# Where the split of silu(gate)*up stands among the weights' splits, and 256 bytes in the place of the sums

## The chip, the cores and the metric

The kernel runs on one core of a Trainium2 chip. The metric is the time of one execution on the device, in microseconds (us). The engines are PE (TensorE, matrix products), DVE (VectorE), ACT (ScalarE), POOL (GpSimd) and SP (SyncE, which here issues the loads). PEld stands for PE's loading of the stationary operand.

## The reference

Two layers act on 256 tokens of width 2048, all in float32. A layer is a mixer (a gated recurrence and two kinds of attention, projected back) and a feed-forward part; the change lies in the second.

```python
for l in range(DEPTH):                      # 2
    ...
    x = x + mix @ w_out[l]
    h = rmsnorm(x, g_ffn[l])
    x = x + (jax.nn.silu(h @ w_gate[l]) * (h @ w_up[l])) @ w_down[l]
return rmsnorm(x, g_final)
```

`w_gate` and `w_up` are 2048 x 5632, `w_down` is 5632 x 2048.

## The kernel before

**Products in three parts.** A float32 product is made of three faster ones: each operand is split into a high part (a cast, `fp32r`) and a low part (the operand less its high part), and `mm3` (lines 234 to 236) adds high x high, high x low and low x high. So each weight tile that arrives from memory in a raw buffer (`wraw`, 6 buffers) is cast by ACT (`whi`, line 228) and subtracted by DVE (`wlo`, line 229) in `load_split`, with 3 buffers for the two parts (`whl_p`). Every activation is split likewise (`split_scaled`: ACT line 399, DVE line 400).

**The feed-forward part.** The 5632 columns are worked in blocks of 512, 11 to a layer, in groups of 4, 4 and 3. A block is one call of `gate_up`; after a group, its part of the down product (`gemm` with `w_down`) is added to `x`. There are 22 blocks in all.

**A block** runs over the 2048 rows in 8 pairs of 256.

- The *ordinary part* takes the first five pairs (`NORD`): 24 products of 128x512 each, `acc<-whi,xTh` and the like in the profile.
- The *sums part* takes the last three pairs with a Strassen-like scheme, seven `mm3` in place of eight. ACT and DVE form sums of the gate's and the up's weights (lines 340 to 343, into raw buffers) and split them into the arena (ACT lines 338, 339, 346, 348; DVE 344, 345, 347, 349). There are two sets of such places, used in turn, `a = p % 2 * SET` (line 329), each of 7168 elements. The seven products go to banks named P1, C11, C12, P5, P7, P6 and C21, in this order. P5, P7 and P6 are taken from a pool of three PSUM banks, `aux` (line 325).
- At its end DVE and ACT form silu(gate)*up from the banks (lines 356 to 380) into `sil`.

**`hidden`** (line 965) turns `sil` into the down product's stationary operand `hT`. For each half it takes an `aux` bank, lets PE make four 128x128 transposes into it (line 393), and splits the bank into `hTh` (ACT, line 399) and `hTl` (DVE, line 400). It is a side job: `run` calls `tick` after each pair of whatever runs next, and `hidden` waits two ticks, so the two halves come after the third and the fourth pair of the next block. After the last block of a group they come after the third and fourth tile of the down product.

**What sets the order of work.** PE's order is written out by hand (`manual_schedule`, line 1015): it is the order of the program text with its ticks. The orders of ACT and DVE are chosen when the program is built, among the instructions that are ready by then, by priority: those within `tc.high_priority(offset=AHEAD)` go ahead of the others, and among equals the earlier in the text. The weights' splits (line 227), the sums (line 337) and the block's closing steps have this priority; `hidden` has not. Each engine then works through its own order without a change on the chip.

The pool that matters:

```python
aux_p = pool("aux", 3, space=PSUM)                 # line 69
P5, P7, P6 = (aux() for _ in range(3))             # line 325
```

Of the kernel before, what the change touches and what calls it, by code (L numbers as in the profile page):

```python
# [21 lines left out]
P = 128  # L22
D = 2048
T = 256
NT = 2
# [8 lines left out]
AHEAD = 100000  # L34
# [23 lines left out]
def body(ctx: ExitStack, tc: tile.TileContext, x_in, pos_in, pvec_in, lamv_in, cst_in, w_in, w_r, w_i, w_q_b,  # L58
# [78 lines left out]
    A_ON = A_RG + 1024 + 1536  # L137
    A_DQ = A_QT

    SET = 7168  # L140
    A_SIL = ARENA1
    A_U = A_SIL + 1024

    def at(a, *shape):
        n = math.prod(shape)
        v = ar1[0][:, a:a + n] if a < ARENA1 else ar2[:, a - ARENA1:a - ARENA1 + n]
        if len(shape) == 2:
            v = v.rearrange("p (a b) -> p a b", a=shape[0])
        elif len(shape) == 3:
            v = v.rearrange("p (a b c) -> p a b c", a=shape[0], b=shape[1])  # L150
        return v
# [54 lines left out]
    def load(src_ap, kk, shape, raw=None):  # L206

        n = kk * math.prod(shape)
        if raw is None:
            raw = wraw_p.tile([P, CHUNK], F32, name="wraw")  # L210
        if len(shape) == 1:
            last_load[:] = [nc.sync.dma_start(raw[:, :n].rearrange("p (k c) -> p k c", k=kk),
                                              src_ap.rearrange("(k p) c -> p k c", p=P))]
        else:
            rv = raw[:, :n].rearrange("p (k h e) -> p k h e", k=kk, h=shape[0])
            sv = src_ap.rearrange("(k p) h e -> p k h e", p=P)
            for k in range(kk):
                nc.sync.dma_start(rv[:, k], sv[:, k])
        return raw
# [78 lines left out]
    def gate_up(wg, wu, rs, sil):  # L298
# [3 lines left out]
        fl = lambda v: v.rearrange("p a b -> p (a b)")  # L302
# [10 lines left out]
        for p in range(NORD):  # L313
            ks = (2 * p, 2 * p + 1)
            hl = [load_split(w[2 * p * P:(2 * p + 2) * P], 2, (512,)) for w in (wg, wu)]
            for s, t in ((0, 0), (1, 1), (0, 1), (1, 0)):
                hi, lo = hl[s]
# [8 lines left out]
        n = KD // 2  # L326
        for p in range(NORD, n):
            ks = (2 * p, 2 * p + 1)
            a = p % 2 * SET
            G, U = (load(w[2 * p * P:(2 * p + 2) * P], 2, (512,)).rearrange("p (a b) -> p a b", a=2)  # L330
                    for w in (wg, wu))
            V, W = (wraw_p.tile([P, CHUNK], F32, name="wraw").rearrange("p (a b) -> p a b", a=2) for _ in range(2))
            gh, gl = at(a, 2, 512), at(a + 1024, 2, 512)
            uh, ul = at(a + 2048, 512), at(a + 2560, 512)
            vh, vl = at(a + 3072, 2, 512), at(a + 4096, 2, 512)
            wh, wl = at(a + 5120, 2, 512), at(a + 6144, 2, 512)
            with tc.high_priority(offset=AHEAD):
                nc.scalar.copy(fl(gh), fl(G))  # L338
                nc.scalar.copy(uh, U[:, 1])
                tt(V[:, 0], U[:, 0], G[:, 0], ALU.subtract)  # L340
                tt(V[:, 1], U[:, 1], U[:, 0], ALU.subtract)  # L341
                tt(W[:, 0], U[:, 1], V[:, 0], ALU.subtract)  # L342
                tt(W[:, 1], G[:, 1], W[:, 0], ALU.subtract)  # L343
                tt(fl(gl), fl(G), f_(fl(gh)), ALU.subtract)  # L344
                tt(ul, U[:, 1], f_(uh), ALU.subtract)  # L345
                nc.scalar.copy(fl(vh), fl(V))  # L346
                tt(fl(vl), fl(V), f_(fl(vh)), ALU.subtract)
                nc.scalar.copy(fl(wh), fl(W))  # L348
                tt(fl(wl), fl(W), f_(fl(wh)), ALU.subtract)  # L349
            first, end = p == NORD, p == n - 1  # L350
            q = p - NORD
            S = [(xSh[:, q, i], xSl[:, q, i]) for i in range(4)]
            mm3(P1, xp(ks[0], 0), (gh[:, 0], gl[:, 0]), first, end)
            if end:
                with tc.high_priority(offset=AHEAD):
                    nc.scalar.copy(sil[1], P1)
            mm3(C11, xp(ks[1], 0), (gh[:, 1], gl[:, 1]), False, end)
            if end:
                with tc.high_priority(offset=AHEAD):
                    tt(sil[0], sil[1], C11, ALU.add)  # L360
                    nc.scalar.activation(sil[0], sil[0], AF.Silu, scale=rs[:, 0:1])
            mm3(C12, S[3], (uh, ul), False, end)
            mm3(P5, S[0], (vh[:, 0], vl[:, 0]), first, end)
            mm3(P7, S[2], (vh[:, 1], vl[:, 1]), first, end)
            mm3(P6, S[1], (wh[:, 0], wl[:, 0]), first, end)
            if end:
                with tc.high_priority(offset=AHEAD):
                    tt(u2, sil[1], P6, ALU.add)
                    tt(u3, u2, P7, ALU.add)
            mm3(C21, xp(ks[1], 1), (wh[:, 1], wl[:, 1]), False, end)  # L370
            if end:
                with tc.high_priority(offset=AHEAD):
                    tt(sil[1], u3, C21, ALU.add)
                    nc.scalar.activation(sil[1], sil[1], AF.Silu, scale=rs[:, 1:2])
                    tt(u2, u2, P5, ALU.add)
                    tt(u2, u2, C12, ALU.add)
                    tt(u3, u3, P5, ALU.add)
                    tt(u3, u3, o22, ALU.add)
                    for t, u in ((0, u2), (1, u3)):
                        nc.vector.scalar_tensor_tensor(sil[t], u, rs[:, t:t + 1], sil[t], ALU.mult, ALU.mult)  # L380
            yield
# [7 lines left out]
    def transposed(dsts, srcs):  # L389

        ps = aux()
        for d, s in zip(dsts, srcs):
            nc.tensor.transpose(ps[:, d:d + P], s, ident)  # L393
        return ps

    def split_scaled(hi, lo, src, g):

        if g is None:
            i = nc.scalar.copy(hi, src)
            nc.vector.tensor_tensor(lo, src, hi.bitcast(F32), ALU.subtract)  # L400
        else:
            i = nc.scalar.activation(hi, src, AF.Copy, scale=g)
            nc.vector.scalar_tensor_tensor(lo, src, g, hi.bitcast(F32), ALU.mult, ALU.subtract)  # L403
        return i
# [161 lines left out]
    def layer(l, rs):  # L566
# [3 lines left out]
        fl = lambda v: v.rearrange("p b t -> p (b t)")  # L570
# [231 lines left out]
        for i in range(4):  # L802
            h = ht_p.tile([P, 4, T], F32R, name="hTh")
            lo = ht_p.tile([P, 4, T], F32R, name="hTl")
            for j in range(4):

                k = (list(range(10, 16)) + list(range(6)) + list(range(6, 10)))[i * 4 + j]
# [148 lines left out]
        for f0, f1 in ((0, 4), (4, 8), (8, 11)):  # L956
            hT = []
            for f in range(f0, f1):
                sil = [at(A_SIL + t * 512, 512) for t in range(NT)]
                fs = slice(f * 512, (f + 1) * 512)  # L960
                run(gate_up(w_gate[l][:, fs], w_up[l][:, fs], rs[0], sil))
                h = ht_p.tile([P, 4, T], F32R, name="hTh")
                lo = ht_p.tile([P, 4, T], F32R, name="hTl")

                def hidden(sil=sil, h=h, lo=lo):
                    yield 2
                    for k in range(0, 4, 2):
                        ps = transposed([0, 128, 256, 384],
                                        [sil[t][:, (k + j) * P:(k + j + 1) * P] for j in range(2) for t in range(NT)])
                        split_scaled(fl(h[:, k:k + 2]), fl(lo[:, k:k + 2]), ps, None)  # L970
                        yield
                add(hidden())
                for j in range(4):
                    hT.append((h[:, j, :], lo[:, j, :]))
            last = f1 == 11
            if end and last:
                take(F32)
                gf = at(0, D)
                nc.sync.dma_start(gf, g_final.to_broadcast([P, D]))
            for cg in range(2):  # L980
                fin = end and last and cg == 1

                def ev(s, t, g, ps):
                    c = cg * 1024 + g * 512
                    nc.vector.tensor_tensor(x[:, t, c:c + 512], x[:, t, c:c + 512], ps, ALU.add)
                    if last:
                        sumsq(ss[:, t, cg * 2 + g:cg * 2 + g + 1], x[:, t, c:c + 512])
                    if end and last and cg == 0:
                        nc.vector.tensor_tensor(x[:, t, c:c + 512], x[:, t, c:c + 512], gf[:, c:c + 512], ALU.mult)
                    if fin and g == 1:  # L990
                        finish(t, ss, gf)
                run(gemm(lambda k: hT[k],
                         [(w_down[l][f0 * 512:f1 * 512, cg * 1024:(cg + 1) * 1024], [(0, 512), (512, 512)])],
                         [[k] for k in range(4 * (f1 - f0))], ev, last=3 if fin else 0))
                drain()
                if last and not end:
                    add(xT_steps("g_mix", l + 1, cg * 8, cg * 8 + 8))
# [62 lines left out]
```

## Time and profile before

| | |
|---|---|
| median of 3 runs | 2241.07 us (2236.26 to 2241.4) |
| the profiled execution's own time | 2241.19 us |
| its span, first to last instruction | 2239.4 us |
| mean granted clock of TensorE | 0.974 |
| moved by DMA | 391.17 MB, mean 175 GB/s |

The profile is of one execution. Its time is 1.8 us above its span, and within 0.2 us of the median. A group's line counts instructions of one line of the code; "idle before" is the time in which the engine had nothing to do just before them, and the releaser is the work whose end let them go. In the rows of a window stand the stretch and its length, then for PE, PEld, DVE, ACT and POOL the busy time (and the count of instructions), then the granted clock as a share of full speed, the mean busy share of the DMA engines and what they moved.

### The profile page before, as it was taken

The numbers are of one execution on the slowest core, as the hardware profiler recorded it, in microseconds if no ns is written. First come the engines' busy times: TensorE is split into PE (matmuls) and PEld (weight loads), VectorE is DVE, ScalarE is ACT, GpSimd is POOL, SyncE is SP. The second block draws the span as 40 slices with busy tenths as digits, with TensorE's granted clock in tenths as the row PEclk, the third lists the DMA queues.
The fourth block names the chain that finished last, engine by engine and source line by source line (L and its number), as shares of the span: only waits on it lengthen the run. The fifth ranks groups of instructions, "written<-read, shape, count | busy, mean of one in ns | idle before, by whom it ended". The sixth has DMA issues, their size and how long they took to land.

```text
span 2239.4 us, 27021 instructions
## 1 busy us (share of the span) xinstructions
PE 2108.8 (94%) x10104; PEld 1761.2 (79%) x10104; DVE 1545.2 (69%) x2115; ACT 1136.2 (51%) x1541; POOL 14.9 (1%) x32
## 2 busy tenths in 40 slices
PE   8999999888998889988999999998889988899888
PEld 8899887777887778877898898877778877788776
DVE  5775658777477774777566756587764877648775
ACT  5854656444354443444447545564543554434444
POOL 0000000000000000000000000000000000000000
PEclk9999999999999999999999999999999999999999
DMA  7564555545664555554565645654556645565553
GB/s 240 167 184 132 170 182 160 175 160 170 193 199 162 169 168 190 180 195 150 175 189 159 179 149 163 183 169 151 173 184 191 195 160 160 186 191 191 169 191 133
DMA packets 183220, 391.17 MB, mean 175 GB/s; under 512 B 18960, under 2 KB 36384, under 8 KB 182960
## 3 DMA queue, kind: packets, MB, share of 16 engines
q1 hardware_dynamic: 183040, 389.36, 54.9%
q8 instruction: 79, 1.29, 0.2%
q14 instruction: 53, 0.43, 0.1%
q0 software_dynamic: 48, 0.09, 0.0%
HBM read 387.30 MB, written 2.10 MB: 174 GB/s over the span
## 4 chain that ended last, share of the span: by engine, by line
PE 69%; DVE 17%; DMA 8%; issue 4%; ACT 2%; SPq 0%; DVEq 0%; POOLq 0%; POOL 0%; ACTq 0%
PE acc L235 20%; PE acc L234 20%; PE acc L236 20%; DMA wraw<-in_w_up 5%; DVE wlo L229 4%; PE aux L234 2%; DVE arena L344 2%; PE aux L235 2%; PE aux L236 2%; DVE arena L349 2%; ACT whi L228 1%; PE aux L393 1%; DVE arena L345 1%; DVE wraw L342 1%; DVE wraw L343 1%
## 5 line engine op out<-in xcount | busy, mean ns | idle before, releaser
L229 DVE TENSOR_TENSOR wlo<-wraw,whi 128x1024 fp32r<-128x1024 f32 (+2 forms) x608 | 716.1, 1182 | 451.5 <-ACT whi L228 446.2
L228 ACT CAST whi<-wraw 128x1024 fp32r<-128x1024 f32 (+2 forms) x608 | 618.7, 1019 | 728.4 <-PE acc L236 536.2
L235 PE MATMUL acc<-wlo,xTh 128*128 128x512 f32 (+1 forms) x1200 | 465.7, 388 | 11.3 <-DVE wlo L229 11.2
L234 PE MATMUL acc<-whi,xTh 128*128 128x512 f32 (+1 forms) x1200 | 471.1, 393 | 0.0
L236 PE MATMUL acc<-whi,xTl 128*128 128x512 f32 (+1 forms) x1200 | 463.5, 386 | 0.0
L234 PE MATMUL acc<-whi,hTh 128*128 128x512 f32 (+1 forms) x992 | 388.2, 391 | 0.0
L236 PE MATMUL acc<-whi,hTl 128*128 128x512 f32 (+1 forms) x992 | 384.7, 388 | 0.0
L235 PE MATMUL acc<-wlo,hTh 128*128 128x512 f32 (+1 forms) x992 | 384.4, 387 | 0.0
L235 PEld LDWEIGHTS acc<-wlo,xTh 128*128 128x128 f32 x1200 | 225.5, 188 | 65.7 <-DVE wlo L229 23.0
L234 PEld LDWEIGHTS acc<-whi,xTh 128*128 128x128 f32 x1200 | 225.4, 188 | 43.9 <-ACT whi L228 0.5
L236 PEld LDWEIGHTS acc<-whi,xTl 128*128 128x128 f32 x1200 | 225.3, 188 | 44.1
L234 PEld LDWEIGHTS acc<-whi,hTh 128*128 128x128 f32 x992 | 186.4, 188 | 37.8 <-issue 1.3
L236 PEld LDWEIGHTS acc<-whi,hTl 128*128 128x128 f32 x992 | 186.2, 188 | 37.9
L235 PEld LDWEIGHTS acc<-wlo,hTh 128*128 128x128 f32 x992 | 186.4, 188 | 36.4
L234 PE MATMUL aux<-arena,xSh 128*128 128x512 f32 x198 | 83.1, 420 | 100.6 <-DVE hTl L400 76.0
L234 PEld LDWEIGHTS aux<-arena,xSh 128*128 128x128 f32 x198 | 38.8, 196 | 114.1 <-ACT whi L228 93.2
L234 PE MATMUL acc<-xTh,whi 128*128 128x256 f32 x384 | 111.1, 289 | 1.7 <-ACT whi L228 1.0
L235 PE MATMUL acc<-xTl,whi 128*128 128x256 f32 x384 | 108.8, 283 | 1.6 <-DVE xTl L403 1.6
L236 PE MATMUL acc<-xTh,wlo 128*128 128x256 f32 x384 | 108.6, 283 | 0.5 <-DVE wlo L229 0.5
L346 ACT CAST arena<-wraw 128x1024 fp32r<-128x1024 f32 x66 | 69.3, 1049 | 47.6 <-DVE wraw L341 47.4
L344 DVE TENSOR_TENSOR arena<-wraw,arena 128x1024 fp32r<-128x1024 f32 x66 | 80.7, 1223 | 14.4 <-ACT arena L338 13.8
L348 ACT CAST arena<-wraw 128x1024 fp32r<-128x1024 f32 x66 | 69.4, 1051 | 36.3 <-DVE wraw L343 28.7
(230 smaller groups left out, 2614.5 us busy)
## 6 DMA issues: line engine op xcount, KB each, us to landing
wraw<-in_w_gate SPq DMA_DIRECT2D x176, 512.0 KB, 4.4
wraw<-in_w_up SPq DMA_DIRECT2D x176, 512.0 KB, 4.6
wraw<-in_w_down SPq DMA_DIRECT2D x176, 512.0 KB, 4.3
wraw<-in_w_out SPq DMA_DIRECT2D x64, 512.0 KB, 3.8
wraw<-in_w_in SPq DMA_DIRECT2D x48, 512.0 KB, 4.0
wraw<-in_w_in SPq DMA_DIRECT2D x48, 384.0 KB, 3.2
wraw<-in_w_in SPq DMA_DIRECT2D x32, 416.0 KB, 3.5
arena<-in_w_in SPq DMA_DIRECT2D x16, 384.0 KB, 7.4
```

What stands on the lines that cost most here:

```text
L228: nc.scalar.copy(hi[:, :n], raw[:, :n])
L229: nc.vector.tensor_tensor(lo[:, :n], raw[:, :n], hi[:, :n].bitcast(F32), ALU.subtract)
L234: nc.tensor.matmul(ps, a[0], b[0], start=start, stop=False)
L235: nc.tensor.matmul(ps, a[0], b[1], start=False, stop=False)
L236: nc.tensor.matmul(ps, a[1], b[0], start=False, stop=stop)
L342: tt(W[:, 0], U[:, 1], V[:, 0], ALU.subtract)
L343: tt(W[:, 1], G[:, 1], W[:, 0], ALU.subtract)
L344: tt(fl(gl), fl(G), f_(fl(gh)), ALU.subtract)
L345: tt(ul, U[:, 1], f_(uh), ALU.subtract)
L346: nc.scalar.copy(fl(vh), fl(V))
L348: nc.scalar.copy(fl(wh), fl(W))
L349: tt(fl(wl), fl(W), f_(fl(wh)), ALU.subtract)
```

## The change

It does two things. `hidden`'s transposes and splits are put within the same high priority that the weights' splits have. And the two sets of sums in the arena begin 64 elements (256 bytes) later: `a` goes from 0 and 7168 to 64 and 7232, counted from the arena's start; the arena has 14,504 elements.

```diff
--- before.py
+++ after.py
@@ -137,7 +137,7 @@
     A_ON = A_RG + 1024 + 1536
     A_DQ = A_QT
 
-    SET = 7168
+    A_SET, SET = 64, 7168
     A_SIL = ARENA1
     A_U = A_SIL + 1024
 
@@ -326,7 +326,7 @@
         n = KD // 2
         for p in range(NORD, n):
             ks = (2 * p, 2 * p + 1)
-            a = p % 2 * SET
+            a = A_SET + p % 2 * SET
             G, U = (load(w[2 * p * P:(2 * p + 2) * P], 2, (512,)).rearrange("p (a b) -> p a b", a=2)
                     for w in (wg, wu))
             V, W = (wraw_p.tile([P, CHUNK], F32, name="wraw").rearrange("p (a b) -> p a b", a=2) for _ in range(2))
@@ -965,9 +965,11 @@
                 def hidden(sil=sil, h=h, lo=lo):
                     yield 2
                     for k in range(0, 4, 2):
-                        ps = transposed([0, 128, 256, 384],
-                                        [sil[t][:, (k + j) * P:(k + j + 1) * P] for j in range(2) for t in range(NT)])
-                        split_scaled(fl(h[:, k:k + 2]), fl(lo[:, k:k + 2]), ps, None)
+                        with tc.high_priority(offset=AHEAD):
+                            ps = transposed([0, 128, 256, 384],
+                                            [sil[t][:, (k + j) * P:(k + j + 1) * P] for j in range(2)
+                                             for t in range(NT)])
+                            split_scaled(fl(h[:, k:k + 2]), fl(lo[:, k:k + 2]), ps, None)
                         yield
                 add(hidden())
                 for j in range(4):
```

## Rows read from the trace of the kernel before

**Rows 1.** Page, part 1: busy us (share of the span) x instructions of each engine

```profile
PE 2108.8 (94%) x10104; PEld 1761.2 (79%) x10104; DVE 1545.2 (69%) x2115; ACT 1136.2 (51%) x1541; POOL 14.9 (1%) x32
```

**Rows 2.** Waits: engine, line, what it waited for: us in total, times, longest

```profile
PE aux L234 <- DVE hTl L400: 76.0, 12, 7.3
...
PE aux L234 <- ACT whi L228: 24.6, 4, 6.6
```

**Rows 3.** Groups by shape: instructions xcount | busy us, mean ns | idle before, releaser

```profile
L229 DVE TENSOR_TENSOR wlo<-wraw,whi 128x1024 fp32r<-128x1024 f32 x508 | 619.0, 1223 | 401.0 <-ACT whi L228 396.4
L228 ACT CAST whi<-wraw 128x1024 fp32r<-128x1024 f32 x508 | 533.9, 1052 | 632.9 <-PE acc L236 500.9 <-issue 59.8 <-DMA wraw<-in_w_gate 21.1
...
L234 PE MATMUL aux<-arena,xSh 128*128 128x512 f32 x198 | 83.1, 420 | 100.6 <-DVE hTl L400 76.0 <-ACT whi L228 24.6
...
L344 DVE TENSOR_TENSOR arena<-wraw,arena 128x1024 fp32r<-128x1024 f32 x66 | 80.7, 1223 | 14.4 <-ACT arena L338 13.8
...
L348 ACT CAST arena<-wraw 128x1024 fp32r<-128x1024 f32 x66 | 69.4, 1051 | 36.3 <-DVE wraw L343 28.7 <-PE acc L236 5.4
...
L400 DVE TENSOR_TENSOR hTl<-aux,hTh 128x512 fp32r<-128x512 f32 x44 | 30.1, 685 | 0.0
...
L399 ACT CAST hTh<-aux 128x512 fp32r<-128x512 f32 x44 | 25.4, 578 | 0.0
```

**Rows 4.** Timeline, 404 to 425 us: start, us, engine, instruction [idle before, releaser]

```profile
406.64 0.60 PE L393 MATMUL aux<-ident,arena 128*128 128x128 f32 x4
...
409.28 0.58 ACT L399 CAST hTh<-aux 128x512 fp32r<-128x512 f32 x1
...
409.70 0.69 DVE L340 TENSOR_TENSOR wraw<-wraw 128x512 f32<-128x512 f32 x1 [0.18 <-DMA wraw<-in_w_up]
...
415.72 0.39 PE L236 MATMUL aux<-arena,xSl 128*128 128x512 f32 x1
416.12 0.69 DVE L340 TENSOR_TENSOR wraw<-wraw 128x512 f32<-128x512 f32 x1
...
420.27 1.23 DVE L347 TENSOR_TENSOR arena<-wraw,arena 128x1024 fp32r<-128x1024 f32 x1
...
421.40 0.69 DVE L400 TENSOR_TENSOR hTl<-aux,hTh 128x512 fp32r<-128x512 f32 x1
...
422.24 0.77 PE L234 MATMUL aux<-arena,xSh 128*128 128x512 f32 x1 [6.13 <-DVE hTl L400]
```

**Rows 5.** Window 409.70 to 421.40, DVE alone: busy us (instructions), clock, DMA share, GB/s

```profile
409.70:421.40 11.70, 11.70 (x15) 0.99 0.60 182
```

**Rows 6.** Timeline around a wait put down to line 228, 808.9 to 810.2 us

```profile
809.02 0.69 DVE L400 TENSOR_TENSOR hTl<-aux,hTh 128x512 fp32r<-128x512 f32 x1
...
809.86 0.76 PE L234 MATMUL aux<-arena,xSh 128*128 128x512 f32 x1 [6.02 <-ACT whi L228]
```

**Rows 7.** Windows around the first wait: us, five engines' busy us, clock, DMA share, GB/s

```profile
416.10:422.24 6.14, 0.01 (x2) 0.03 (x1) 6.14 (x10) 3.14 (x3) 0.00 (x0) 0.90 0.78 220
422.24:427.90 5.66, 5.66 (x13) 4.44 (x14) 4.57 (x4) 2.09 (x2) 0.00 (x0) 0.50 1.04 378
```

**Rows 8.** Windows: sums parts of the 16 blocks with the wait, first and sum

```profile
412.55:435.86 23.31, 17.18 (x65) 13.67 (x63) 15.43 (x19) 9.07 (x10) 0.00 (x0) 0.85 0.63 211
...
sum 364.68, PE 264.11 PEld 210.92 DVE 249.23 ACT 146.81 POOL 0.00; mean PE 16.51 PEld 13.18 DVE 15.58 ACT 9.18 POOL 0.00
```

**Rows 9.** Windows: sums parts without it, first of a layer, and sum of four others

```profile
365.47:381.12 15.65, 14.57 (x65) 11.75 (x63) 14.59 (x23) 10.34 (x13) 0.00 (x0) 1.00 0.58 188
...
sum 57.11, PE 57.11 PEld 47.31 DVE 55.35 ACT 37.51 POOL 0.00; mean PE 14.28 PEld 11.83 DVE 13.84 ACT 9.38 POOL 0.00
```

**Rows 10.** Windows: ordinary parts after ten with, four without, and a layer's first

```profile
sum 282.57, PE 282.57 PEld 232.37 DVE 233.21 ACT 154.98 POOL 0.00; mean PE 28.26 PEld 23.24 DVE 23.32 ACT 15.50 POOL 0.00
...
sum 117.55, PE 114.77 PEld 92.62 DVE 99.48 ACT 63.40 POOL 0.00; mean PE 28.69 PEld 23.16 DVE 24.87 ACT 15.85 POOL 0.00
...
381.12:412.55 31.43, 29.26 (x130) 22.99 (x129) 26.69 (x32) 17.15 (x20) 0.00 (x0) 1.00 0.59 187
```

## The prediction

> **What bounds the kernel now.** I read the page's first part, then the waits, then the groups of the long wait, then the order in time around one of its occurrences, then all occurrences side by side. The first part puts PE at 94% of the span, DVE at 69% and ACT at 51% [rows 1]: PE carries the time, and its idle 130 us are the place to look. The waits say that most of that idle time stands in one place, PE's `aux` product of line 234: 12 waits for the split `hTl` of line 400, 76.0 us, and 4 put down to line 228, 24.6 us [rows 2]; its group shows the same 100.6 us [rows 3]. That is 16 waits of 6.3 us.
>
> The order in time shows what one of them is [rows 4]. PE runs the three pairs of the Strassen-like part (below "the sums part") from 412.55. After P5 and P7 of the first pair, at 415.72, comes P6, which takes the third `aux` bank. That bank still holds the second four transposes of the block before, made at 406.64. ACT copied them to `hTh` at 409.28, but DVE subtracts them to `hTl` only at 421.40: fifteen instructions of the next two pairs' sums stand in DVE's order ahead of it, from L340 at 409.70 to L347 at 420.27 [rows 5]. PE starts again at 422.24, 0.15 us after `hTl` ends. The four waits put down to line 228 are the same: at 809.86 PE starts 0.15 us after an `hTl` that began at 809.02 and took 0.69 [rows 6]. So all 16 end with this one instruction.
>
> The wait costs more than its idle time. Cutting that block into stretches, the granted clock is 0.90 on the mean while PE is idle and 0.50, the lower of its levels of 1.2 and 2.4 GHz, for the 5.66 us after it [rows 7]. So the whole of the sums part is the right measure. The 16 blocks with the wait take 364.68 us, 22.79 each, at a clock of 0.85 [rows 8]. In the first block of a group no earlier block has left transposes, and the wait is missing: four of the six such blocks take 57.11 us, 14.28 each, at a clock of 1.00, all of it PE's busy time [rows 9]. The other two, the first of each layer, take 15.65.
>
> **The change, part by part.**
>
> *Priority of `hidden`.* It adds and removes no instruction. PE's order is written by hand, so the transposes stay where they are; 44 `hTh` copies (0.58 us) and 44 `hTl` splits (0.69 us) [rows 3] get the standing of the weights' splits. In ACT's order they already sit next to the transposes (409.28 against 406.64 [rows 4]). In DVE's order `hTl` should go from 421.40 to right behind `hTh`, near 410. The instructions that it passes, of two pairs, start one `hTl`, at most 0.69 us, later. They issue no DMA; what SP issues when DVE frees a raw buffer is later by that 0.69 too, and POOL has no work here. Then P6's bank is free some 5 us before PE asks for it, PE doesn't stop, and the clock doesn't fall. Each block saves 22.79 - 14.28 = 8.51 us, of which 6.3 is idle time and 2.2 the low clock: 16 x 8.51 = **136.2 us**.
>
> *What is late next.* Without the wait DVE and the DMAs lose the time in which they got ahead. Is the last pair's data there? DVE doesn't stop during the wait, so its times hold: `vl` of the third pair (L347) is done at 420.27 + 1.23 = 421.50. PE, without a stop, would want it at 412.55 + 2 x 4.76 + 3 x 0.68 = 424.1 (4.76 is a third of 14.28, 0.68 a seventh of that). Slack 2.6 us, less the 0.69 that `hTl` takes. Nothing new stops PE there, as in the free blocks.
>
> After that comes the next block's ordinary part, with less lead. After a block with the wait it takes 28.26 us (282.57 over 10); after a free block 117.55 over 4, 29.39 [rows 10], because the weights' low parts come late behind the block's closing sums. Ten of the 16 blocks are followed by a further block: 10 x 1.13 = **11.3 us** given back. Six are followed by the down product, where PE has twelve products of 0.227, 2.7 us, for each new weight tile: I take nothing, and keep 6 x 1.13 = 6.8 us as the bound.
>
> A page speaks against the whole gain. The Trainium skill, "Perfetto Trace Analysis", section "Optimization Strategy", reads a gap that repeats on the engine that should be saturated as a possible sign that SBUF or PSUM is too small for the next tile. By that reading three `aux` banks are too few, a new order alone leaves the gap, and the time stays. The trace says otherwise to me: a free bank here lacks only a subtraction whose input was there 11.5 us before.
>
> *The 256 bytes.* Nothing in the trace of before shows a cost of where the sums lie. The casts and splits into the sums take 1051 (L348) and 1223 ns (L344), those into the weight tiles 1052 (L228) and 1223 (L229) [rows 3]. PE's 63 products that read the sums take 14.28 / 63 = 0.227 us each in a free block; five ordinary pairs have 120 products from the weight tiles and two sets of transposes of 0.60 [rows 4] in 28.26: 0.226. A difference of 3 ns on some 400 such instructions would be 1 us, so I take 0, and keep 1 us either way. The last set now ends at element 14,400 of the arena's 14,504, so it runs into nothing.
>
> **Sum.** 2239.4 - 136.2 + 11.3 = 2114.5 us of span; the profiled execution's own time is 1.8 above its span and 0.1 above the median of the runs: **2116 us**, 5.6% less.
>
> **The rivals.**
>
> *The wait moves to the weights.* DVE is close to full, and every block now follows a fast one. The dearest case in the trace is the first block of a layer, where DVE starts with no lead: 15.65 [rows 9] and then 31.43 [rows 10], in place of 14.28 and 29.39. If every block were so: 10 x 3.41 + 6 x 1.37 = 42 us back, 2158. For it: DVE is busy 55.35 of 57.11 us in the free blocks [rows 9]. Against it: in the ordinary part it is busy 99.48 of 117.55 [rows 10], so it can catch up in each block, and the loads ran at 378 GB/s when they had to [rows 7].
>
> *The order doesn't change, or the banks are too few whichever it is.* The placing of `hTl` is decided when the program is built, by a model of the engines' times; if there it isn't ready before the sums, it stays late. Then 2241. That would need `hTh` late too, and it isn't: it is there 2 us after the transposes. The skill's reading above would give this time as well.
>
> *Slower: ACT or DVE stands waiting for the transposes.* `hTh` and `hTl` are put into ACT's and DVE's order ahead of the next pair's casts, PE reaches the transposes later than the model thought, and the casts queue behind. Its place is the end of the third and fourth ordinary pair. After each transpose PE then waits for `hTh`, `whi` and `wlo` in turn, 0.58 + 1.05 + 1.22 = 2.85 us [rows 3], twice a block: 5.7. The sums start without lead, and DVE needs 6.42 us for a pair (from L340 at 409.70 to L340 at 416.12 [rows 4]) against PE's 4.76: 1.6 late at the last pair, and two splits of 1.13 (from L347 at 420.27 to the next start at 421.40) behind it, 2.3. Together 9.6 us a block, 154 us: 2116 + 154 = 2270. It decides from 7.8 us a block (124.9 / 16) on. Against it: ACT shows no wait before `hTh` in the rows, and the sums of a later pair are begun at 409.70, ahead of PE's first product with any at 412.55. The Trainium skill, "PSUM — Partial Sum Buffer", section "Engine vs sequencer instructions", says that ScalarE's and VectorE's queues are strictly first in, first out, which is what this case needs; the fifteen instructions ahead of a ready `hTl` agree.
>
> **How the numbers follow.** The forecast has 0.76, the wait that moves 0.15, no change 0.05, slower 0.04. A measurement of this kernel can tell about 0.3% from no change. Faster by more is the first two, 0.91; same 0.05; slower 0.04. The range goes from the sum without what is given back (2105), with 5 us of room for the sums' place and the small waits elsewhere, 2100, to the moved wait with the down products' 6.8 us, 2165. It leaves out the last two cases and little more.
>
> **What would show it.** In the new profile `hTl` starts within some 5 us of the transposes. The group of line 234 with `aux` and `xSh` has under 10 us of idle time, from 100.6. The 16 sums parts take 14.3 to 15 us, at a clock of 1.00. The ordinary parts take 29 to 30. PE is busy near 98%. The casts and splits of the sums keep 1051 and 1223 ns. It is wrong if `hTl` is early and the sums parts still take over 16 us, or the ordinary parts over 31 (the wait has moved); if `hTl` is still behind the sums (nothing was reordered); or if `hTh` has idle time of ACT before it (slower).

## The result, and the profile after

The changed kernel takes 2115.9 us (median; 2114.2 to 2118.2) against 2239.1 of the kernel before beside it: a ratio of 0.945, with a 95% interval of 0.9435 to 0.9467. The forecast was 2116. The profiled execution's span is 2114.5 us, 124.9 less than before; the mean granted clock went from 0.974 to 0.999.

Part 1 of the page of the changed kernel, which answers to [rows 1]:

```profile
PE 2078.1 (98%) x10104; PEld 1738.2 (82%) x10104; DVE 1539.4 (73%) x2115; ACT 1132.4 (54%) x1541; POOL 14.9 (1%) x32
```

The same work in fewer us: PE has 36 us idle in place of 131, and 31 us less busy time, since its products no longer run at the low clock.

The groups of the changed kernel by shape, which answer to [rows 3]:

```profile
L229 DVE TENSOR_TENSOR wlo<-wraw,whi 128x1024 fp32r<-128x1024 f32 x508 | 618.0, 1223 | 390.0 <-ACT whi L228 386.4
...
L344 DVE TENSOR_TENSOR arena<-wraw,arena 128x1024 fp32r<-128x1024 f32 x66 | 80.6, 1222 | 14.9 <-ACT arena L338 14.8
...
L234 PE MATMUL aux<-arena,xSh 128*128 128x512 f32 x198 | 77.0, 389 | 0.0
...
L348 ACT CAST arena<-wraw 128x1024 fp32r<-128x1024 f32 x66 | 69.6, 1054 | 61.4 <-DVE wraw L343 61.0
```

The third line is the one to see: its idle time went from 100.6 us to 0.0, and its mean from 420 to 389 ns. The casts and splits of the sums kept their 1051 and 1223 ns to within 3.

The order in time around the same place as [rows 4], in two stretches:

```profile
406.45 0.60 PE L393 MATMUL aux<-ident,arena 128*128 128x128 f32 x4
...
408.07 0.58 ACT L399 CAST hTh<-aux 128x512 fp32r<-128x512 f32 x1
...
409.34 0.68 DVE L400 TENSOR_TENSOR hTl<-aux,hTh 128x512 fp32r<-128x512 f32 x1
...
410.24 0.69 DVE L340 TENSOR_TENSOR wraw<-wraw 128x512 f32<-128x512 f32 x1 [0.21 <-DMA wraw<-in_w_up]
...
415.53 0.39 PE L236 MATMUL aux<-arena,xSl 128*128 128x512 f32 x1
...
415.75 0.39 PE L234 MATMUL aux<-arena,xSh 128*128 128x512 f32 x1
...
420.81 1.22 DVE L347 TENSOR_TENSOR arena<-wraw,arena 128x1024 fp32r<-128x1024 f32 x1
```

`hTl` now follows the transposes by 2.9 us, ahead of L340, and P6 (415.75) follows P7 (its last product at 415.53) at once: the bank was free 5.7 us before. The last pair's L347 ends at 422.03, and PE wants it at 412.35 + 9.52 + 2.04 = 423.9: 1.9 us of slack, which is the predicted 2.6 less 0.69.

The windows of the changed kernel over the 16 sums parts that had the wait, first and sum, which answer to [rows 8]:

```profile
412.35:426.63 14.28, 14.28 (x64) 11.83 (x63) 14.28 (x17) 8.89 (x11) 0.00 (x0) 1.00 0.66 220
...
sum 228.49, PE 228.49 PEld 189.21 DVE 228.11 ACT 141.87 POOL 0.00; mean PE 14.28 PEld 11.83 DVE 14.26 ACT 8.87 POOL 0.00
```

364.68 - 228.49 = 136.2 us saved, at a clock of 1.00. DVE is now busy in 228.11 of 228.49 us.

The windows over the ten ordinary parts behind them, last and sum, to [rows 10]:

```profile
1994.46:2024.30 29.84, 28.54 (x130) 23.15 (x128) 25.50 (x32) 16.40 (x19) 0.00 (x0) 1.00 0.58 195
sum 289.78, PE 286.25 PEld 231.53 DVE 243.67 ACT 156.63 POOL 0.00; mean PE 28.62 PEld 23.15 DVE 24.37 ACT 15.66 POOL 0.00
```

282.57 became 289.78: 7.2 us given back, half of it idle time (289.78 - 286.25 = 3.5). Nearly all of the other half, which counts as busy, is waiting too. A product is shown with 0.39 us while the next starts 0.23 us after it, so a short delay leaves PE busy. PE's loads of the operand show the delay. In these ten parts they wait 2.3 us for `wlo` before and 10.6 after; in the whole kernel, before and then after:

```profile
PEld acc L235 <- DVE wlo L229: 23.0, 33, 1.6
```

```profile
PEld acc L235 <- DVE wlo L229: 30.0, 43, 1.7
```

From start to start, the 400 products of the ten parts that read `wlo` (line 235) follow the one before by 0.246 us on the mean, in place of 0.233: 5.5 of the 7.2 us. Those of line 235 and of line 236, which comes next, make up 6.9.

The windows from the end of a last block of a group to the next group's first sums part, four of six (a down product of some 88 us, and the ordinary part behind it), the sum of before and then that of after:

```profile
sum 463.11, PE 462.02 PEld 381.23 DVE 270.79 ACT 194.86 POOL 0.00; mean PE 115.51 PEld 95.31 DVE 67.70 ACT 48.72 POOL 0.00
```

```profile
sum 466.99, PE 463.21 PEld 380.94 DVE 275.26 ACT 195.84 POOL 0.00; mean PE 115.80 PEld 95.23 DVE 68.81 ACT 48.96 POOL 0.00
```

Another 3.9 us are given back there, all of it in the down products. What PE now waits for near the start of a down product stands in the order in time, and then in the waits (changed kernel):

```profile
515.19 0.69 DVE L373 TENSOR_TENSOR arena<-arena,acc 128x512 f32<-128x512 f32 x1
...
515.93 0.50 PE L234 MATMUL acc<-whi,hTh 128*128 128x512 f32 x1 [0.73 <-DVE arena L373]
```

```profile
PE acc L234 <- DVE arena L373: 3.5, 6, 1.2
```

The down product begins at 513.00; its tenth product is the first into the bank of C21, which the closing step of line 373 is still reading. In the kernel before there is no such wait. So 136.2 - 7.2 - 3.9 = 125.1 are accounted for, of the span's 124.9. In the rest, the six parts behind a first block got 1.2 us shorter and everything else 1.4 longer.

### The profile page after: what moved, and what is told of

It is laid out like the page before. It is cut to its first block, busy times and chain, and to the rows that moved or that the text cites. A ratio compares the mean times of both kernels' runs of the same rounds, so it can differ in the third digit from the quotient of the medians.

```text
span 2114.5 us, 26989 instructions
## 1 busy us (share of the span) xinstructions
PE 2078.1 (98%) x10104; PEld 1738.2 (82%) x10104; DVE 1539.4 (73%) x2115; ACT 1132.4 (54%) x1541; POOL 14.9 (1%) x32
## 3 DMA queue, kind: packets, MB, share of 16 engines
q8 instruction: 79, 1.29, 0.3%
## 4 chain that ended last, share of the span: by engine, by line
PE 59%; DVE 25%; DMA 9%; issue 4%; ACT 2%; DVEq 0%; SPq 0%; POOLq 0%; ACTq 0%; POOL 0%
PE acc L235 18%; PE acc L236 18%; PE acc L234 18%; DVE wlo L229 7%; DMA wraw<-in_w_up 5%; DVE arena L344 2%; DMA wraw<-in_w_gate 2%; DVE wraw L341 2%; DVE arena L349 2%; DVE wraw L342 2%; ACT whi L228 2%; PE aux L393 1%; DVE wraw L343 1%; DVE wraw L340 1%; DVE arena L345 1%
## 5 line engine op out<-in xcount | busy, mean ns | idle before, releaser
L348 ACT CAST arena<-wraw 128x1024 fp32r<-128x1024 f32 x66 | 69.6, 1054 | 61.4 <-DVE wraw L343 61.0
L346 ACT CAST arena<-wraw 128x1024 fp32r<-128x1024 f32 x66 | 69.5, 1053 | 49.8 <-DVE wraw L341 49.8
L344 DVE TENSOR_TENSOR arena<-wraw,arena 128x1024 fp32r<-128x1024 f32 x66 | 80.6, 1222 | 14.9 <-ACT arena L338 14.8
L338 ACT CAST arena<-wraw 128x1024 fp32r<-128x1024 f32 x66 | 69.3, 1050 | 23.8 <-DMA wraw<-in_w_gate 23.5
L349 DVE TENSOR_TENSOR arena<-wraw,arena 128x1024 fp32r<-128x1024 f32 x66 | 80.7, 1222 | 0.2
```

## The experiments

The theory: a single instruction, the second half's `hTl`, stood too late in DVE's order, it held P6's bank, and each wait cost its idle time and the low clock after it. The rivals are named with each experiment. Each ratio is to the kernel before, run beside it.

**The two parts of the change apart.** First the priority alone:

```diff
-    A_SET, SET = 64, 7168
+    A_SET, SET = 0, 7168
```

> The priority without the 256 bytes (the sums stay at 0 and 7168). Theory (the order of hTl carries everything): the time of the changed kernel, 2116 us within 0.3% (2110 to 2122), sums parts 14.28 us, idle time before the aux products under 10 us. Rival (the place of the sums carries a part): over 2122, by as much as the place carries, and casts or splits of the sums or PE's products on them longer than 1.05, 1.22 and 0.227 us.

Measured: 2115.8 us, ratio 0.9444 (0.9431 to 0.9457); the 16 sums parts take 14.28 us on the mean, with no idle time before the `aux` products of line 234.

Then the 256 bytes alone:

```diff
-    SET = 7168
+    A_SET, SET = 64, 7168
...
-            a = p % 2 * SET
+            a = A_SET + p % 2 * SET
```

> The 256 bytes without the priority. Theory: the time of the kernel before, 2239 us within 0.3% (2232 to 2246), with its 16 waits, some 100 us, before P6. Rival (the place carries a part): under 2232, with the same waits but shorter casts, splits or products.

Measured: 2239.6 us, ratio 0.9996 (0.9987 to 1.0005). Its groups:

```profile
L234 PE MATMUL aux<-arena,xSh 128*128 128x512 f32 x198 | 83.1, 420 | 99.3 <-DVE hTl L400 86.9 <-ACT whi L228 12.4
...
L344 DVE TENSOR_TENSOR arena<-wraw,arena 128x1024 fp32r<-128x1024 f32 x66 | 80.6, 1222 | 14.1 <-ACT arena L338 14.0
...
L348 ACT CAST arena<-wraw 128x1024 fp32r<-128x1024 f32 x66 | 69.4, 1052 | 37.0 <-DVE wraw L343 28.5 <-PE acc L236 6.2
```

The wait is all there. In this run, of the wait for the one instruction, 12.4 us are put down to line 228, 24.6 in [rows 2]: the share of the two names is no property of the kernel. The 256 bytes are worth nothing that can be told, and the rival of the place falls.

**One half alone.** In the kernel before:

```diff
+from contextlib import ExitStack, nullcontext
...
-                        split_scaled(fl(h[:, k:k + 2]), fl(lo[:, k:k + 2]), ps, None)
+                        with (tc.high_priority(offset=AHEAD) if k == 2 else nullcontext()):
+                            split_scaled(fl(h[:, k:k + 2]), fl(lo[:, k:k + 2]), ps, None)
```

> The split of the second four transposes alone gets the priority; the transposes' calls and the first half stay as before; no 256 bytes. Theory (the one late instruction is the second half's hTl, which holds P6's bank): all of the gain, 2113 to 2122, no wait before P6. Rival (PE needs both halves early, P7's bank being the first half's): a wait before P7 takes the place of the one before P6, some us in each of 16 blocks, and the time stays over 2150.

Measured: 2113.4 us, ratio 0.9432 (0.9420 to 0.9445). The order in time shows the two `hTl` of a block, and the second product of each of P5, P7 and P6 in their turn:

```profile
402.71 0.60 PE L393 MATMUL aux<-ident,arena 128*128 128x128 f32 x4
...
408.62 0.69 DVE L400 TENSOR_TENSOR hTl<-aux,hTh 128x512 fp32r<-128x512 f32 x1
408.67 0.60 PE L393 MATMUL aux<-ident,arena 128*128 128x128 f32 x4
...
411.49 0.68 DVE L400 TENSOR_TENSOR hTl<-aux,hTh 128x512 fp32r<-128x512 f32 x1
...
416.87 0.39 PE L235 MATMUL aux<-arena,xSh 128*128 128x512 f32 x1
...
417.55 0.39 PE L235 MATMUL aux<-arena,xSh 128*128 128x512 f32 x1
...
418.23 0.39 PE L235 MATMUL aux<-arena,xSh 128*128 128x512 f32 x1
```

The first half's split stays 5.9 us behind its transposes (408.62 against 402.71), which harms nothing; the second's comes 2.8 us behind, and PE takes the three banks 0.68 us apart. So the second half alone carries the gain. The edit moves its `hTh` along with its `hTl`, but in the kernel before `hTh` was done at 409.86, 11.5 us ahead of the `hTl` for which PE waited, so it is the `hTl` that counts. The ten ordinary parts take 28.59 us in place of 28.98, so the first half's early place seems to cost 0.4 us each; in the time this is within the two intervals.

**The price of the low clock.** The kernel before, with work for PE in the wait:

```diff
-            mm3(P6, S[1], (wh[:, 0], wl[:, 0]), first, end)
+            [nc.tensor.matmul(P7, warm[:, 0:P], warm, start=False, stop=False) for _ in range(26 * (first and pad))]; mm3(P6, S[1], (wh[:, 0], wl[:, 0]), first, end)
...
-                run(gate_up(w_gate[l][:, fs], w_up[l][:, fs], rs[0], sil))
+                run(gate_up(w_gate[l][:, fs], w_up[l][:, fs], rs[0], sil, f > f0))
```

> The kernel before, and in each of the 16 blocks with the wait 26 more products of an all-zero tile by itself (bf16, 512 columns, added into P7's bank, so nothing changes in it) ahead of P6: PE works through most of the wait, 26 x 0.21 = 5.6 of 6.3 us, and every other engine has its order as before. Theory (2.2 of the 8.5 us that a wait costs are the low clock after it): the granted clock stays at 1.00, the sums parts go from 22.79 to 20.6 us, and the time from 2239 to 2204 (2196 to 2212). Rival (the 2.2 us are something else, as DVE or the DMAs catching up): the sums parts stay at 22.8 and the time at 2239, or above by what the products run over.

Measured: 2207.6 us, ratio 0.9854 (0.9841 to 0.9867), 33 us less than before for 416 more products. Its windows over the 16 sums parts, first and sum:

```profile
412.48:432.93 20.45, 20.13 (x89) 14.22 (x89) 15.10 (x18) 9.06 (x10) 0.00 (x0) 1.00 0.69 240
...
sum 329.75, PE 321.74 PEld 227.40 DVE 244.38 ACT 145.17 POOL 0.00; mean PE 20.11 PEld 14.21 DVE 15.27 ACT 9.07 POOL 0.00
```

The parts take 20.61 us, 2.18 less than the 22.79 of before, at a clock of 1.00 where it was 0.85. The wait itself is as long as it was (20.61 - 14.28 = 6.3). So of a wait's 8.5 us, 2.2 are the low clock behind it, and the rival falls.

**How much room there is.** Two doses on the changed kernel. First the transposes one pair later:

```diff
-                    yield 2
+                    yield 3
```

> The changed kernel with hidden's two halves one pair later, after the fourth and the fifth pair, so that the second half's transposes end as the sums part begins. Theory (what counts is only that hTl is done before PE reaches P6, 3.4 us into the sums part): hTl follows the transposes by 3 us, which is just in time; 2114 to 2126, waits before P6 under 0.7 us each. Rival (the early place in the order was needed for more than this bank): some us in each of 16 blocks, over 2140.

Measured: 2121.3 us, ratio 0.9473 (0.9454 to 0.9491). The waits of this run in which line 400 or `aux` products stand:

```profile
PEld aux L235 <- DVE arena L347: 3.1, 2, 1.6
...
PE aux L235 <- DVE arena L347: 2.3, 2, 1.2
...
PEld aux L234 <- DVE hTl L400: 2.0, 3, 1.0
```

PE's loading for P6 waited for `hTl` in three of 16 blocks, 2.0 us in all, as the theory had it: just in time is nearly as good as early.

Then more work for DVE at the same place:

```diff
                             split_scaled(fl(h[:, k:k + 2]), fl(lo[:, k:k + 2]), ps, None)
+                            tt2 = [nc.vector.tensor_tensor(fl(lo[:, k:k + 2]), ps, fl(h[:, k:k + 2]).bitcast(F32), ALU.subtract) for _ in range(2)]
```

> The changed kernel with each hTl split done three times over (the same values written again): 4 x 0.69 = 2.8 us more of DVE's time in each block. Theory (DVE has room: some 4 us idle in an ordinary part, 2 us of lead at the last pair): at most 1 us a block shows, 2116 to 2138. Rival (the wait has moved to DVE, which is now the bound): all of it shows, 16 x 2.8 = 44 us, about 2160.

Measured: 2144.3 us, ratio 0.9581 (0.9564 to 0.9597), 28.4 us over the changed kernel: of 2.8 us a block 28.4 / 16 = 1.8 show. Both expectations miss. The waits of this run:

```profile
PEld acc L235 <- DVE wlo L229: 43.7, 53, 1.9
PE acc L235 <- DVE wlo L229: 25.2, 26, 1.5
...
PEld acc L234 <- DVE arena L373: 12.9, 6, 2.2
...
PE acc L234 <- DVE arena L373: 10.3, 6, 1.7
PEld aux L235 <- DVE arena L349: 8.9, 16, 0.8
```

PE waits a little at the last sums (L349), and most for the next block's `wlo` and for L373. The 2 us of slack at the last pair are there, but DVE has no idle time from the second `hTl` to the closing steps, so what is put in there comes out behind them. DVE's room is about 1 us a block.

**Where the given-back time comes from.** First, three closing steps to other engines:

```diff
-                    tt(u3, u3, o22, ALU.add)
+                    nc.gpsimd.tensor_tensor(u3, u3, o22, ALU.add)
                     for t, u in ((0, u2), (1, u3)):
-                        nc.vector.scalar_tensor_tensor(sil[t], u, rs[:, t:t + 1], sil[t], ALU.mult, ALU.mult)
+                        nc.scalar.activation(u, u, AF.Copy, scale=rs[:, t:t + 1])
+                        nc.gpsimd.tensor_tensor(sil[t], u, sil[t], ALU.mult)
```

> The changed kernel, and three of a block's closing steps leave DVE: the sum of line 378 and the two last products of line 380 go to POOL, with the scaling of line 380 to ACT. Theory (what is given back, 7 us in the ordinary parts, comes from DVE's closing steps standing ahead of the next block's weights): 1.9 us of the burst leave DVE, the ordinary parts after a sums part go from 28.98 to 28.4 to 28.7 us, and the time to 2106 to 2113. Rival (they come from the loads, or from DVE's total): the parts stay at 29.0 and the time at 2116; and where POOL's steps slow DVE's, which run at the same time, above it.

Measured: 2144.9 us, ratio 0.9585 (0.9568 to 0.9602), 29 us slower than the changed kernel. Its order in time behind a sums part:

```profile
431.69 1.29 POOL L378 TENSOR_TENSOR arena<-arena 128x512 f32<-128x512 f32 x1 [40.69 <-DVE arena L377]
433.02 1.34 ACT L380 ACTIVATE arena<-arena,rs 128x512 f32<-128x512 f32 x2 [1.91 <-POOL arena L378]
433.82 2.51 POOL L381 TENSOR_TENSOR arena<-arena 128x512 f32<-128x512 f32 x2 [0.84 <-ACT arena L380]
434.26 1.98 ACT L228 CAST whi<-wraw 128x1024 fp32r<-128x1024 f32 x2
...
435.32 3.22 DVE L229 TENSOR_TENSOR wlo<-wraw,whi 128x1024 fp32r<-128x1024 f32 x2 [3.18 <-ACT whi L228]
435.34 0.50 PE L234 MATMUL acc<-whi,xTh 128*128 128x512 f32 x1 [0.68 <-ACT whi L228]
...
437.47 0.50 PE L235 MATMUL acc<-wlo,xTh 128*128 128x512 f32 x1 [1.62 <-DVE wlo L229]
```

ACT's scaling has the weights' priority and stands ahead of the next cast, but has to wait for POOL (1.91 us); the cast of line 228 queues behind it, `wlo` behind that, and PE waits. It is the prediction's third rival, on a step that I moved myself. A second thing adds to it: the first of the two splits of line 229, beside POOL's products (433.82 to 436.33), took 2.09 us, and the second, mostly behind them, 1.21. By an estimate from these two, PE's wait of 1.62 us would have been 0.9 shorter without it (2.09 - 1.21). Over the run the 508 splits of this shape take 639.8 us, in place of 618.0. How the 29 us divide between the two wasn't measured. As a test of the closing steps it says nothing.

So the same three steps were left on DVE, out of the priority:

```diff
-                    tt(u3, u3, o22, ALU.add)
-                    for t, u in ((0, u2), (1, u3)):
-                        nc.vector.scalar_tensor_tensor(sil[t], u, rs[:, t:t + 1], sil[t], ALU.mult, ALU.mult)
+                tt(u3, u3, o22, ALU.add)
+                for t, u in ((0, u2), (1, u3)):
+                    nc.vector.scalar_tensor_tensor(sil[t], u, rs[:, t:t + 1], sil[t], ALU.mult, ALU.mult)
```

> The changed kernel with the last three closing steps of a block (lines 378 and 380, which read no bank) out of the high priority, so that DVE may take the next block's weights first; POOL and ACT keep their order. Theory (what is given back comes from DVE's closing steps ahead of the weights' low parts): the first ordinary pairs no longer wait for wlo, the ten ordinary parts go from 28.98 to 28.4 to 28.8 us, and the time to 2107 to 2113. Rival (it comes from the loads or from PE itself): 28.9 to 29.1, and 2116 within 0.2%.

Measured: 2110.2 us, ratio 0.9421 (0.9409 to 0.9434). The time is as expected, but its place is not. The order changed mainly in the first blocks of the groups: the six ordinary parts behind these, last and sum, of the changed kernel and then of this one:

```profile
1950.98:1980.18 29.20, 28.74 (x130) 23.16 (x128) 23.54 (x29) 14.70 (x17) 0.00 (x0) 1.00 0.56 180
sum 179.25, PE 172.85 PEld 138.61 DVE 150.95 ACT 96.03 POOL 0.00; mean PE 28.81 PEld 23.10 DVE 25.16 ACT 16.00 POOL 0.00
```

```profile
1945.87:1974.12 28.25, 28.25 (x130) 23.16 (x128) 23.73 (x30) 14.77 (x18) 0.00 (x0) 1.00 0.57 183
sum 174.95, PE 171.68 PEld 138.79 DVE 152.25 ACT 96.94 POOL 0.00; mean PE 28.61 PEld 23.13 DVE 25.37 ACT 16.16 POOL 0.00
```

4.3 us come from these six; the ten others take 28.93 in place of 28.98. In all six at least one step of line 380 now stands behind two splits of the next weights. Five of them are shorter, the last from 29.20 to 28.25, as fast as any; one is not (29.28 in place of 29.13). So closing steps ahead of the weights do cost time in the parts behind a first block. In the ten, DVE's order from the first closing step to the next weights is the same in both traces: there the edit moved nothing, and the theory is untested.

**Both finds together**, on the kernel before: the second half's priority alone, and the three closing steps out of it.

> The kernel with the second half's priority alone (2113 us there), and the same three closing steps out of the high priority. If both help by themselves, 2104 to 2110; if the second is nothing, 2113 within 0.2%.

Measured: 2106.1 us, ratio 0.9404 (0.9391 to 0.9417), clear of the changed kernel's 0.9435 to 0.9467. It is faster than both kernels.

## Why the prediction was right

Point by point, by its steps:

- **The cause and its place.** Right, and shown: with the second half's splits alone moved, the whole gain is there.
- **8.51 us a block, 136.2 in all.** Right: 136.2 by the windows. The step that measured a whole part, and not the idle time, carried it: the 100.6 us of the waits would have given 26% too little. That 2.2 us of each block are the clock is shown by the products put into the wait.
- **The last pair's slack.** Right: 1.9 us, as worked out.
- **The given-back 11.3 us.** The sum is right by luck: two errors cancel. The ten ordinary parts gave back 7.2 and not 11.3. They take 28.98, not the 29.39 of a part behind a first block, which was the wrong model for them. The down products, taken at nothing, gave back 3.9 over four of six. The step that failed is that a down product is safe because it wants one tile in 2.7 us: it isn't short of weights, it wants the bank that line 373 still reads. The bound of 6.8 held, with 5.3 at most (3.9, and the 1.4 of everything else).
- **The 256 bytes.** Right: 0.9996, with 0.9987 to 1.0005.
- **The rival of the moved wait.** Wrong as an outcome, but nearer than its 0.15 said. I argued that DVE's idle time in the ordinary part lets it catch up. That lead is spent before the sums are done: in the sums parts DVE is busy 228.11 of 228.49 us, and 1.8 of the 2.8 us put into a block come out.
- **The rival of too few banks**, which the Trainium skill's reading of repeated gaps ("Perfetto Trace Analysis", section "Optimization Strategy") stood beside: it falls. The gap went from 100.6 to 0.0 us with three banks as before.
- **The slower rival.** It didn't happen here. Its mechanism is real, as the closing steps on POOL and ACT show: ACT waits 1.91 us there and PE after it. Of the 29 us over the changed kernel this is a part; DVE's slower splits beside POOL are another.

What stays open is why `wlo` comes late in the ten ordinary parts. In the first of them (changed kernel) the trace points to the closing steps: the cast of line 228 is done at 432.02, and its `wlo` starts at 432.92, when DVE is through with line 380. But no run moved these steps there. The loads could have a share as well: they take more of the DMA engines beside these parts (0.57 in that part, against 0.41 in the same part of the kernel before), and no run separates the two. The difference of 2.5 us between the second half's priority alone and the change as it is lies within the intervals.

## What to carry to other kernels

When an engine waits again and again for a small step of another, look where that step stands in the other engine's order and what is ahead of it, before adding a buffer: here a split of 0.69 us that was ready 11.5 us early, behind fifteen others, cost 136 us in 16 places. Price such a wait by comparing the same stage with and without it, since the low clock behind a gap added a third to its idle time here (2.2 to 6.3 us). And give the priority to the one step that holds what is waited for: every other step that gets it, above all one that must itself wait for a further engine, stands ahead of the work that the priority was meant for.

## What was not expected of the hardware

- Products of an all-zero tile, put into the wait, kept the granted clock at 1.00 in it and in the 5.7 us behind it, where it had stood at 0.50.
- POOL's 128x512 sum took 1.29 us where DVE's takes 0.69. Two of DVE's splits, the first of them beside POOL's two products, took 3.22 us together, and 2.36 in the changed kernel.
